# A four-layer decoder trunk on one core: the compressed branch of sparse attention in one 128x128 square under a rearranged plan, and differential attention pinned piece by piece

## The chip, the cores and the metric

The kernel runs on 1 core of one Trainium2 chip. The metric is device time in microseconds (us): the median of three runs of the kernel before is 2169.16 us (2161.97 to 2175.18). The engines of the core are TensorE (PE, matrix multiplications; PEld are its weight loads), VectorE (DVE), ScalarE (ACT), GpSimd (POOL) and SyncE (SP, which issues most DMAs). Each executes its own instructions in the order in which they were queued; they meet at semaphores.

## The reference

`x` is [1, 256, 1024], float32. Four layers, each `x + FFN_a/2`, `x + Mixer`, `x + FFN_b/2`, with norms and scales computed from a vector `c`. The mixers are NSA (layers 0 and 3), stick-breaking (layer 1) and differential attention (layer 2). Cut to the parts that the change touches:

```python
# NSA, compressed branch (15 blocks of 32 tokens; 16 heads in 4 groups)
s = einsum('bqgrd,bngd->bgrqn', q, k_cmp) * scale
s = where(dist >= 0, s - slopes * dist, NEG)             # dist = t - block end
p_cmp = softmax(s) * valid
o_cmp = einsum('bgrqn,bngd->bqgrd', p_cmp, v_cmp)
o = g[..., 0:1] * o_cmp + g[..., 1:2] * o_sel + g[..., 2:3] * o_win
return o @ w_out
# differential attention (8 heads, two maps each)
p = softmax(s - slopes * dist)
a = p[:, :, 0] - lam_full * p[:, :, 1]
o = rms_norm(einsum('bhqk,bkhe->bqhe', a, v), subln_g) * (1 - lam_init)
return o @ w_out
```

## The kernel before

Every weight matrix is streamed from memory in pieces and split into a high part (ScalarE, L135) and a low part (VectorE, L136); a product is three matmuls (high by high, low by high, high by low). One `lo_wo` or `lo_w` is such a VectorE subtraction of 128x1024. TensorE alternates between FFN stages and mixer stages. In the profiled execution NSA of layer 0 lies at 219 to 405 us of the span, NSA of layer 3 at 1803 to 1983, differential attention at 1291 to 1430.

A mixer is worked in four Attend pieces `a`, `b`, `c`, `d`: `a` and `b` hold the first eight heads for the first and the second 128 tokens, `c` and `d` the other eight (`HALVES`). In NSA each piece has the steps `S` (scores of two branches, L927; VectorE adds the distances and finds the row maximum with a fused custom instruction at L936; ScalarE takes the exponential; VectorE scales at L948), `T` (TensorE transposes the weights, ScalarE copies them as `pT`, L956 to L958), `P` (multiplied by the values, L909), `C` (compressed scores, L971, and their softmax on VectorE, L972 to L985), `D` (eight transposes of the compressed weights, 15 columns each, and two copies, L685 and L631), `E` (two matmuls with the compressed values `vc`) and `put` (output to `yh` and `yl`, L627 and L628). `q`, `kc`, `hid`, `cout`, `cout_T` make the projections and the compressed keys and values; `weight k` loads and splits a piece of the output weights, `o h k` multiplies by it.

The step strings in `plan` fix TensorE's order: `pin` (L304) makes each step's instructions come after the last matmul of the step before. The other engines' queues are laid by the scheduler from what TensorE's order and the data leave open. `bank` names three groups of PSUM banks: `acc` (4), `mm` (2; scores of `S` and `C`) and `tp` (2; transposes, and the projections in `cout_T`). A step that needs a bank waits until the last reader of that bank's previous content is done; so does one that needs an `s2` buffer (6, `NS2`).

Differential attention (`Diff`, a `Dense`) is not pinned: `plan` orders generator calls, and the scheduler mixes their instructions on TensorE: projections `proj`, `heads` (scores, L663, maximum L666), `second` (transposes L1145, values L1150), the normed output's transposes (`p_ot`, L1170) and `out_proj`.

Of the kernel before, what the change touches and what calls it, by code (L numbers as in the profile page):

```python
# [21 lines left out]
FT = mybir.dt.float32  # L22
FR = mybir.dt.float32r
BF = mybir.dt.bfloat16
AF = mybir.ActivationFunctionType
# [3 lines left out]
D = 1024  # L29
# [11 lines left out]
def trunk_kernel(ctx, tc, x, c, ada_w, ada_b, norm_g, ffn_w1, ffn_w2, nsa_w_in, nsa_cmp_pe, nsa_cmp_w1,  # L41
# [581 lines left out]

    def put_o(p, k0, h):

        tok = slice(h * 128, (h + 1) * 128)
        nc.scalar.copy(yh[:, k0:k0 + 4, tok], p)  # L627
        nc.vector.tensor_sub(yl[:, k0:k0 + 4, tok], p, yh[:, k0:k0 + 4, tok])  # L628
# [63 lines left out]
    class Nsa(Mixer):  # L692
        W = D + 6 * 256 + 48
        plan = """gate; q 0 0; gate_T; S a 0; q 0 2; S b 0 0; q 0 3; S b 0 1; kc 0 0; S a 1; T a 0 0; T a 0 1; kc 0 1;
                  P a 0 0; P a 0 1; kc 1 0; T b 0 0; T b 0 1; kc 1 1; P b 0 0; T b 0 2; q 1 4 0; P b 0 1; T b 0 3; q 1 4 1;
                  P b 0 2; P b 0 3; S b 1 0; q 1 5; S b 1 1; T a 1 0; T a 1 1; hid 0; P a 1 0; P a 1 1; S c 0; hid 1; weight 0;
                  hid 2; weight 1; hid 3; T b 1 0; T b 1 1; weight 2; q 1 2; P b 1 0; T b 1 2; weight 3; q 1 3 0; P b 1 1; T b 1 3; cout; q 1 3 1;
                  P b 1 2; P b 1 3; cout_T; S c 1; C a; T c 0 0; T c 0 1; C b; P c 0 0; P c 0 1; S d 0 0; D a; weight 4;
                  S d 0 1; E a; D b; weight 5; E b; o 0 0; C c; o 0 1; T c 1 0; T c 1 1; weight 6; o 0 2; P c 1 0; P c 1 1; S d 1 0;
                  o 0 3; D c; weight 7; C d; S d 1 1; E c; T d 0 0; T d 0 1; o 0 4; P d 0 0; T d 0 2; o 0 5; P d 0 1; T d 0 3;  # L700
                  o 0 6; P d 0 2; P d 0 3; o 0 7; D d; o 1 0 0; T d 1 0; E d; o 1 1 0; T d 1 1; P d 1 0; o 1 2 0; T d 1 2;
                  P d 1 1; o 1 3 0; T d 1 3; P d 1 2; P d 1 3; put d"""
        rest = """o 1 0 1; o 1 1 1; o 1 2 1; o 1 3 1; o 1 4 0; o 1 5 0; o 1 6 0; o 1 7 0; o 1 4 1; o 1 5 1; o 1 6 1; o 1 7 1"""

        def run(self, plan):


            for op in plan.replace("\n", " ").split(";"):
                op, *args = op.split()
                if args and args[0] in "abcd":  # L710
                    pin(getattr(self.at[args[0]], op), *map(int, args[1:]))
                else:
                    pin(getattr(self, op), *map(int, args))

        def body(self):
            pinned[:] = []
            self.at = {c: self.Attend(self, *half) for c, half in zip("abcd", HALVES)}
            self.run(self.plan)

        def tail(self):  # L720
            self.run(self.rest)
# [116 lines left out]
        def cout(self):  # L838
# [6 lines left out]
            self.hT = hT  # L845

        def cout_T(self):
# [9 lines left out]
            self.vc = work.tile([NCMP, 4, 64], FT, name="vc", tag="vc", bufs=1)  # L857
            p = bank("tp", [NCMP, 4, 64], "p_vc")
            for g in range(4):
                for cc in range(2):  # L860
                    nc.tensor.matmul(p[:, g, :], hT[:, cc, 64 + g * NCMP:64 + (g + 1) * NCMP], self.w2c[:, 1, cc, 0:64],
                                     start=cc == 0, stop=cc == 1)
            nc.scalar.copy(self.vc, p)
# [16 lines left out]
        def weight(self, k):  # L880
            gate_on[:] = self.copied
            self.wo[k] = self.out_weight(k)
            gate_on[:] = []

        def o(self, h, k, n=None):

            ns = (0, 1) if n is None else (n,)
            accs = self.accs.setdefault(h, [None, None])
            for m in ns:
                if accs[m] is None:  # L890
                    accs[m] = bank("acc", [128, 512], f"o{h}{m}")
# [397 lines left out]
```

## Time and profile before

| | us |
|---|---|
| median of three runs | 2169.16 |
| profiled execution | 2169.74 |
| its span | 2167.9 |
| PE busy in it | 2096.4 (97%) |
| DVE busy | 1622.9 (75%) |
| ACT busy | 1119.8 (52%) |
| NSA stage of layer 0, layer 3 | 185.7, 179.2 |
| differential attention | 139.4 |

The rows below come from four views: what TensorE waited for in a stretch, the busy time of the engines in stretches with the granted clock of TensorE (1.00 is 2.4 GHz, 0.50 would be 1.2 GHz throughout), groups of instructions by shape, and single instructions in order of time. In the rows `[1.53 <-DVE sm_m L936]` at the end of a row means that the engine had stood idle for 1.53 us and that the release came from VectorE's L936.

### The profile page before, as it was taken

The page shows a single profiled execution, that of the slowest core. Times are in us where ns is not written, and L with a number is a line of the kernel's source. Part 1 is how long each engine was busy: PE and PEld are TensorE (multiplying, and loading weights), DVE is VectorE, ACT ScalarE, POOL GpSimd, SP SyncE. Part 2 cuts the span into 40 slices and gives each one's busy share as a digit, 9 for nine tenths or more (in the row PEclk, how much of TensorE's full clock was granted, in tenths as well). Part 3 has the DMA queues.
Part 4 walks back from the last instruction along what each step waited for, and adds up shares of the span by engine and source line. Part 5 has one row for each costly group of instructions (what it writes and reads, how often), then busy time and mean ns, then how long its engine had stood idle before and what let it go on. Part 6 is the DMA issues. An engine that isn't in the chain of part 4 may idle for free.

```text
span 2167.9 us, 37376 instructions
## 1 busy us (share of the span) xinstructions
PE 2096.4 (97%) x14395; PEld 1856.1 (86%) x14395; DVE 1622.9 (75%) x2736; ACT 1119.8 (52%) x1989; POOL 67.3 (3%) x154
## 2 busy tenths in 40 slices
PE   5999999999999999999999999999999999999998
PEld 5999775899899979799989888789999997668998
DVE  7987866777798777677688858687779868767654
ACT  3444655644544456754464455664455445656443
POOL 1000000000000000100000000000000000000000
PEclk9999998999999999999999999999999999999999
DMA  9998752687699856388779958278869986545761
GB/s 316 335 348 287 252 137 78 215 287 262 199 330 312 282 186 222 122 278 277 256 235 330 313 170 297 78 240 274 275 203 330 308 276 194 163 118 172 241 200 59
DMA packets 338179, 512.55 MB, mean 236 GB/s; under 512 B 20832, under 2 KB 211256, under 8 KB 338000
## 3 DMA queue, kind: packets, MB, share of 16 engines
q1 hardware_dynamic: 329456, 501.15, 69.9%
q10 hardware_dynamic: 8544, 9.01, 1.4%
q8 instruction: 113, 1.85, 0.3%
q14 instruction: 66, 0.54, 0.1%
HBM read 507.91 MB, written 1.05 MB: 235 GB/s over the span
## 4 chain that ended last, share of the span: by engine, by line
PE 74%; DVE 11%; issue 5%; DMA 5%; ACT 4%; POOL 2%; ACTq 0%; SPq 0%; DVEq 0%; POOLq 0%
PE p_gu L386 12%; PE p_gu L388 12%; PE p_gu L387 12%; PE f L405 6%; PE f L406 6%; PE f L409 6%; DVE lo_w L136 3%; DMA raw_ada<-in_ada_w_dram 3%; PE p_o L909 1%; PE p_pr L386 1%; PE p_pr L387 1%; PE p_pr L388 1%; PE p_t L956 1%; POOL rx L325 1%; PE o L405 1%
## 5 line engine op out<-in xcount | busy, mean ns | idle before, releaser
L135 ACT CAST hi_w<-raw_w 128x1024 fp32r<-128x1024 f32 x528 | 551.5, 1055 | 325.6 <-PE f L409 113.4
L136 DVE TENSOR_TENSOR lo_w<-raw_w,hi_w 128x1024 fp32r<-128x1024 f32 x528 | 633.1, 1221 | 103.6 <-ACT hi_w L135 97.2
L386 PE MATMUL p_gu<-yh,hi_w 128*128 128x256 f32 x2368 | 665.6, 281 | 4.0 <-DVE yh L351 4.0
L387 PE MATMUL p_gu<-yl,hi_w 128*128 128x256 f32 x2368 | 660.9, 279 | 0.3 <-DVE yl L352 0.3
L388 PE MATMUL p_gu<-yh,lo_w 128*128 128x256 f32 x2368 | 661.0, 279 | 0.0
L386 PEld LDWEIGHTS p_gu<-yh,hi_w 128*128 128x128 f32 x2368 | 445.7, 188 | 17.3 <-DVE lo_w L136 6.2
L192 DVE SCALAR_TENSOR_TENSOR ada_acc<-raw_ada,cT,ada_acc 128x512 f32<-128x512 f32 x500 | 374.0, 749 | 103.3 <-DMA raw_ada<-in_ada_w_dram 95.3
L387 PEld LDWEIGHTS p_gu<-yl,hi_w 128*128 128x128 f32 x2368 | 446.0, 188 | 5.4 <-issue 1.7
L388 PEld LDWEIGHTS p_gu<-yh,lo_w 128*128 128x128 f32 x2368 | 445.8, 188 | 0.2
L405 PE MATMUL f<-hi_w,hb 128*128 128x512 f32 x704 | 275.8, 393 | 1.9 <-ACT hb L550 1.8
L406 PE MATMUL f<-lo_w,hb 128*128 128x512 f32 x704 | 275.9, 392 | 0.0
L409 PE MATMUL f<-hi_w,hb 128*128 128x512 f32 x704 | 228.3, 391 | 0.0
L550 ACT CAST hb<-sg 128x256 fp32r<-128x256 f32 x148 | 60.2, 407 | 199.6 <-DVE sg L549 198.1
L548 ACT ACTIVATE sg<-p_gu 128x256 f32<-128x256 f32 x148 | 56.3, 380 | 204.1 <-PE p_gu L388 183.8
L405 PEld LDWEIGHTS f<-hi_w,hb 128*128 128x128 f32 x704 | 132.3, 188 | 29.2 <-ACT hb L550 4.7
L409 PEld LDWEIGHTS f<-hi_w,hb 128*128 128x128 f32 x704 | 131.6, 188 | 29.3 <-DVE hb L551 1.9
L406 PEld LDWEIGHTS f<-lo_w,hb 128*128 128x128 f32 x704 | 132.2, 188 | 24.5 <-DVE lo_w L136 0.3
L549 DVE TENSOR_TENSOR sg<-sg,p_gu 128x256 f32<-128x256 f32 x148 | 61.5, 416 | 79.0 <-ACT sg L548 78.8
L551 DVE TENSOR_TENSOR hb<-sg,hb 128x256 fp32r<-128x256 f32 x148 | 62.4, 422 | 35.2 <-ACT hb L550 35.2
L350 ACT ACTIVATE y<-p_y,ab 128x128 f32<-128x128 f32 x184 | 67.2, 465 | 29.7 <-PE p_y L339 24.2
L387 PE MATMUL p_pr<-yl,hi_qk 128*128 128x256 f32 x256 | 71.8, 281 | 0.0
L386 PE MATMUL p_pr<-yh,hi_qk 128*128 128x256 f32 x256 | 71.5, 281 | 0.0
(273 smaller groups left out, 3191.6 us busy)
## 6 DMA issues: line engine op xcount, KB each, us to landing
raw_w<-in_ffn_w_dram SPq DMA_DIRECT2D x528, 512.0 KB
raw_ada<-in_ada_w_dram SPq DMA_DIRECT2D x288, 512.0 KB
raw_kv<-in_nsa_w_in_dram SPq DMA_DIRECT2D x16, 512.0 KB
raw_q<-in_nsa_w_in_dram SPq DMA_DIRECT2D x16, 512.0 KB
raw_cw<-in_nsa_cmp_w_dram SPq DMA_DIRECT2D x16, 512.0 KB
raw_wo<-in_nsa_w_out_dram SPq DMA_DIRECT2D x32, 256.0 KB
raw_qk<-in_sb_w_in_dram SPq DMA_DIRECT2D x16, 512.0 KB
raw_qk<-in_diff_w_in_dram SPq DMA_DIRECT2D x16, 512.0 KB
```

What stands on the lines that cost most here:

```text
L135: nc.scalar.copy(hi, src)
L136: nc.vector.tensor_sub(lo, src, hi)
L192: nc.vector.scalar_tensor_tensor(a, r[:, j], cT[:, k:k + 1], a, op0=OP.mult, op1=OP.add)
L350: nc.scalar.activation(y[:, j, :], p[:, j, :], AF.Identity, scale=ab[:, k:k + 1], bias=ab[:, 8 + k:9 + k])
L386: nc.tensor.matmul(o, cols(wh), yh[:, k, :], start=first and k == 0, stop=False)
L387: nc.tensor.matmul(o, cols(wh), yl[:, k, :], start=False, stop=False)
L388: nc.tensor.matmul(o, cols(wl), yh[:, k, :], start=False, stop=last and k == KC - 1)
L405: nc.tensor.matmul(acc[n], lh, wh[:, sl], start=first, stop=False)
L406: nc.tensor.matmul(acc[n], lh, wl[:, sl], start=False, stop=False)
L409: nc.tensor.matmul(acc[n], ll, wh[:, sl], start=False, stop=last)
L549: nc.vector.tensor_mul(sg, sg, p[:, 1, :])
L551: nc.vector.tensor_sub(hl[:, cc, :], sg, hh[:, cc, :])
```

## The change

It has three parts. (1) The compressed branch works on 16 columns for each of 8 heads, 128 in all, so that `D` is one 128x128 transpose and one copy; `E` becomes eight matmuls against `vz`, which holds the compressed values of a head's group in the rows of that head and zeros elsewhere (built in `cout_T` with the mask `own`). (2) The step string of NSA is rearranged. (3) `Diff` gets such a string, pinned step by step, in place of the generators. Line numbers of the kernel after are higher by 11 to 14 from L909 on.

```diff
 # NSA: cout, cout_T
+            hx = self.hx = s2([128, 2, 4, 4, 16], "hx")
+            nc.gpsimd.memset(hx, 0.0)
+            for cc in range(2):
+                nc.vector.tensor_copy(hx[:, cc, :, :, 0:NCMP], p[:, cc, 64:64 + 4 * NCMP].rearrange(
...
-                    nc.tensor.matmul(p[:, g, :], hT[:, cc, 64 + g * NCMP:64 + (g + 1) * NCMP], self.w2c[:, 1, cc, 0:64],
-            nc.scalar.copy(self.vc, p)
+                    nc.tensor.matmul(p[:, gp, :], self.hx[:, cc, 2 * gp:2 * gp + 2].rearrange("p e r n -> p (e r n)"),
+            for gp in range(2):
+                vz = self.X[0].rearrange("p m e -> p (m e)")[:, gp * 512:(gp + 1) * 512].rearrange("p (a d) -> p a d", a=8)
+                nc.vector.tensor_mul(vz, p[:, gp, None, :].to_broadcast([128, 8, 64]), own[:, :, None].to_broadcast([128, 8, 64]))
 # NSA: C, D, E
-                nc.vector.tensor_mul(m, m, self.nsa.gates[:, h, 8 * gp:8 * gp + 8, 0])
-                if not h:
-                    nc.vector.tensor_mul(pc, pc, cvalid[h][:, None, :].to_broadcast([128, 8, NCMP]))
+                nc.vector.scalar_tensor_tensor(m, m, cvalid[h][:, 0:1], self.nsa.gates[:, h, 8 * gp:8 * gp + 8, 0],
...
-                for e in range(2):
-                    self.ct[e] = transpose4(lambda rr: self.pc[:, 4 * e + rr, :], e)
+                p = bank("tp", [128, 128], "p_ct")
+                nc.tensor.transpose(p, self.pc.rearrange("p a n -> p (a n)"), ident)
+                self.ct = s2([128, 128], "cT")
+                evac(self.h, self.ct, p)
...
-                    self.add(e, slice(0, 4), self.nsa.vc[:, 2 * self.gp + e, :], self.ct[e][:NCMP])
+                for rr in range(4):
+                    for e in range(2):
+                        self.add(e, rr, self.nsa.vz[self.gp][:, 4 * e + rr, :], self.ct)
 # NSA: plan
-        plan = """gate; q 0 0; gate_T; S a 0; q 0 2; S b 0 0; ...
+        plan = """gate; q 0 0; gate_T; q 0 2; S a 0; q 0 3; S b 0 0; ...
 # Diff
-    class Diff(Dense):
+    class Diff(Pinned, Dense):
-        plan = [("proj", 1, 0,), ("proj", 0, 0,), 'a', ("proj", 1, 1,), 'b', 'a', ...
+        plan = """pj 1 0 0; pj 0 0 0; S a 0; pj 1 0 1 0; S b 0; pj 1 0 1 1; ...
...
+                  T c 0; pj 0 1 1 0; P c 0; weight 0; pj 0 1 1 1; N a; S c 1; T d 0; weight 1; N b; S d 1; P d 0; weight 2; o 0 0;
+                  weight 3; T c 1; o 0 1; weight 4; P c 1; T d 1; weight 5; o 0 2; weight 6; P d 1; o 0 3; weight 7; N c;
```

Three places in the instruction order. First TensorE in NSA, from the projections of `cout_T` (`p_kcT`, `p_vc`) to the first output product (`o_...`); `p_s` are the steps `S`, `p_sc` `C`, `p_t` from `sc` `T`, `p_t` from `pc` (after: `p_ct`) `D`, `p_o` from `pT` `P` and, from `vc` or `cT`, `E`. Before:

```order
L853 MATMUL p_kcT<-hT,self.w2c 128x60 x2
L861 MATMUL p_vc<-self.w2c,hT 15x64 x8
L927 MATMUL p_s<-qkv 128x256 x4
L971 MATMUL p_sc<-kc,qkv 128x32 x4
L956 MATMUL p_t<-ident,sc 128x128 x8
L971 MATMUL p_sc<-kc,qkv 128x32 x4
L909 MATMUL p_o<-pT,qkv 64x256 x4
L927 MATMUL p_s<-qkv 128x512 x2
L685 MATMUL p_t<-ident,pc 15x128 x8
L927 MATMUL p_s<-qkv 128x512 x2
L909 MATMUL p_o<-pT,vc 64x512 x2
```

The same stretch after, from the last `P` ahead of the scores of `d`:

```order
L920 MATMUL p_o<-pT,qkv 64x256 x4
L938 MATMUL p_s<-qkv 128x512 x2
L999 MATMUL p_ct<-ident,pc 128x128
L938 MATMUL p_s<-qkv 128x512 x2
L999 MATMUL p_ct<-ident,pc 128x128
L920 MATMUL p_o<-cT,qkv 64x128 x8
L938 MATMUL p_s<-qkv 128x256 x4
L920 MATMUL p_o<-cT,qkv 64x128 x8
L982 MATMUL p_sc<-kc,qkv 128x32 x4
L405 MATMUL o_3839<-hi_wo,yh 128x512
```

The scores `S c 1` (128x256 x4) moved from ahead of the first `C` to between `E a` and `E b`; `T c 0` now comes right behind `cout_T`, `C a` and `C b` stand together, and `C c` comes ahead of the first output product.

Second, VectorE's queue at the same place after: `L947 ISA` is the fused scores instruction (before L936), `L959` the scaling (before L948), `cT` the copy of `D a`, `yl` the output of a piece.

```order
L667 COPY cT<-p_ct 128x128
L136 TENSOR_TENSOR lo_wo<-raw_wo,hi_wo 128x1024
L954 RECIPROCAL sm_r<-sm_l 128x4
L947 ISA sc,sm_m<-p_s,dist 128x256
L947 ISA sm_m 128x1
L955 TENSOR_TENSOR sm_r<-sm_r,gates 128x4
L947 ISA sc,sm_m<-p_s,dist 128x256
L947 ISA sm_m 128x1
L959 TENSOR_SCALAR sc<-sc,sm_r 128x256 x4
L947 ISA sc,sm_m<-p_s,dist 128x256
L947 ISA sm_m 128x1
```

A weight split and four scalings stand between the fused instructions that read the scores of `d`, and the eight 128x128 ones of `S c 1` come behind all of these.

Third, TensorE in differential attention, where the projections are done and the output products begin: `p_ot` transposes a finished piece (step `N`), `p_t` the weights (`T`), `p_o` is the product with the values (`P`). Before:

```order
L1170 MATMUL p_ot<-ident,o_n 128x128 x2
L663 MATMUL p_s<-qkv 128x256 x7
L1170 MATMUL p_ot<-ident,o_n 128x128
L1145 MATMUL p_t<-ident,sc 128x128
L1170 MATMUL p_ot<-ident,o_n 128x128
L1145 MATMUL p_t<-ident,sc 128x128
L663 MATMUL p_s<-qkv 128x256
L1170 MATMUL p_ot<-ident,o_n 128x128 x2
L1150 MATMUL p_o<-qkv,aT 128x128 x2
```

After:

```order
L1220 MATMUL p_ot<-ident,o_n 128x128 x4
L699 MATMUL p_s<-qkv 128x128 x4
L1192 MATMUL p_t<-ident,sc 128x128 x4
L1220 MATMUL p_ot<-ident,o_n 128x128 x4
L699 MATMUL p_s<-qkv 128x256 x4
L1203 MATMUL p_o<-qkv,aT 128x128 x4
L405 MATMUL o_14988<-hi_wo,yh 128x512
```

The two last sets of scores of piece `d`, which stood together (x7 and x1 of 128x256), are apart: four of them here, the other four were moved up between the projections. The output products begin one `N` and one `P` after the last scores.

## Rows read from the trace of the kernel before

**Rows 1.** What TensorE waited for, NSA of layer 0 (219 to 405 us): total, times, longest.
```profile
PE p_o L909 <- DVE pT L631: 2.5, 1, 2.5
PE p_s L927 <- ACT qkv L775: 1.7, 1, 1.7
PE p_sc L971 <- DVE sm_m L936: 1.5, 1, 1.5
PE p_hid L824 <- DMA raw_cw<-in_nsa_cmp_w_dram: 1.0, 1, 1.0
PE p_o L909 <- ACT pT L958: 0.6, 1, 0.6
```

**Rows 2.** The same view, NSA of layer 3 (1803.5 to 1983 us).
```profile
PE p_hid L824 <- DMA raw_cw<-in_nsa_cmp_w_dram: 1.3, 1, 1.3
PE p_s L927 <- ACT qkv L775: 0.7, 1, 0.7
```

**Rows 3.** The same view, differential attention (1290.6 to 1430 us).
```profile
PE p_s L663 <- DVE sm_m L666: 4.3, 3, 2.4
PE o L405 <- ACT yh L627: 0.8, 1, 0.8
```

**Rows 4.** Stretches: length, busy PE, PEld, DVE, ACT, POOL, granted clock, DMA share, GB/s.
```profile
260.00:270.00 10.00, 9.16 (x56) 7.59 (x57) 8.02 (x39) 7.09 (x25) 0.00 (x0) 0.83 0.95 309
328.00:340.00 12.00, 11.35 (x51) 6.80 (x52) 8.94 (x50) 8.64 (x29) 0.00 (x0) 0.72 0.19 60
340.00:356.00 16.00, 13.48 (x51) 9.17 (x49) 9.26 (x33) 5.80 (x15) 0.00 (x0) 0.68 0.22 67
356.00:370.00 14.00, 14.00 (x68) 8.82 (x68) 11.77 (x42) 8.96 (x25) 0.00 (x0) 0.88 0.37 112
1380.00:1392.00 12.00, 9.63 (x41) 6.63 (x40) 9.07 (x36) 6.45 (x29) 1.01 (x1) 0.72 0.32 98
1920.00:1936.00 16.00, 13.48 (x52) 9.95 (x51) 9.00 (x30) 6.63 (x16) 0.00 (x0) 0.68 0.21 67
```

**Rows 5.** TensorE in order of time: `p_ht` and `S d 1 1`, layers 0 and 3.
```profile
321.67 0.38 PE L842 MATMUL p_ht<-ident,th 128*128 128x128 f32 x2
361.29 2.01 PE L927 MATMUL p_s<-qkv 64*128 64x512 f32 x4
...
1903.46 0.38 PE L842 MATMUL p_ht<-ident,th 128*128 128x128 f32 x2
1940.73 1.67 PE L927 MATMUL p_s<-qkv 64*128 64x512 f32 x4
```

**Rows 6.** VectorE by shape, NSA of layer 3: count, busy, mean ns, idle before.
```profile
L936 DVE CUSTOM_DVE_ANT_0 sc<-p_s,dist 128x256 f32<-128x256 f32 x32 | 12.2, 415 | 0.2 <-PE p_s L927 0.2
L136 DVE TENSOR_TENSOR lo_wo<-raw_wo,hi_wo 128x1024 fp32r<-128x1024 f32 x8 | 9.6, 1216 | 6.3 <-ACT hi_wo L135 6.3
L948 DVE TENSOR_SCALAR sc<-sc,sm_r 128x256 f32<-128x256 f32 x32 | 9.1, 347 | 0.2
L936 DVE CUSTOM_DVE_ANT_0 sc<-p_s,dist 128x128 f32<-128x128 f32 x32 | 7.1, 286 | 2.7 <-PE p_s L927 2.7
L628 DVE TENSOR_TENSOR yl<-p_o,yh 128x512 fp32r<-128x512 f32 x4 | 2.7, 684 | 3.7 <-ACT yh L627 3.7
```

**Rows 7.** VectorE in order of time, layer 3: first and last of the nine of `C c`.
```profile
1929.32 0.28 DVE L972 TENSOR_TENSOR pc<-p_sc,cdist 128x120 f32<-128x120 f32 x1 [3.04 <-PE p_sc L971]
...
1931.70 0.28 DVE L985 TENSOR_TENSOR pc<-pc,c_m 128x120 f32<-128x120 f32 x1
```

**Rows 8.** TensorE by shape, NSA of layer 3: `E` and `D` of four pieces.
```profile
L909 PE MATMUL p_o<-pT,vc 15*64 15x512 f32 x16 | 5.0, 640 | 2.5 <-DVE pT L631 2.5
L685 PE MATMUL p_t<-ident,pc 128*15 128x128 f32 x32 | 4.2, 273 | 0.3 <-DVE pc L985 0.3
```

**Rows 9.** TensorE by shape, the whole span: value products of layers 1 and 2.
```profile
L1090 PE MATMUL p_o<-sb_a,qkv 128*64 128x128 f32 x96 | 8.5, 281 | 1.4 <-POOL sb_a L1085 1.3
L1150 PE MATMUL p_o<-qkv,aT 128*128 128x128 f32 x48 | 6.9, 289 | 0.0
```

## What the change will do: the prediction

> **What bounds the kernel now.** I read four views, in this order. First, what TensorE waits for, stage by stage, because it is busy 97% of the span and only its gaps and its clock can be won. In the three stages touched it waits little: in NSA of layer 0 for the copies of the compressed weights (2.5), the first projected queries (1.7), the row maxima of scores (1.5), a weight load (1.0) and a copy of `pT` (0.6) [rows 1]; in layer 3 the 2.5, the 1.5 and the 0.6 are there again, the load takes 1.3 and the queries 0.7 [rows 2]; in differential attention it waits 4.3 for maxima and 0.8 for `yh` [rows 3]. Second, the granted clock: right after these waits it is below 1.00 [rows 4]. A stretch of length L at clock g was at the half level for 2(1-g)L: 3.4, 6.7, 10.2 and 3.4 us in layer 0, 10.2 in layer 3, 6.7 in differential attention. Half-level time costs at most half of itself. Third, VectorE's durations [rows 6, 7], since it is the engine waited for most. Fourth, single matmuls by shape, for what the square adds and removes [rows 8, 9].
>
> **The change part by part.** All is counted in the profiled execution (2169.7; 1.8 of it outside the span, untouched; 0.6 above the median).
>
> *A, the start of NSA.* `q 0 2` now stands between the first projection and `S a 0`. Its weights are those of `q 0 0`, already split, so it starts at once, and its 24 matmuls are longer than the wait for the queries. Layer 0 gains 1.7 [rows 1] and half of the 3.4 us at the half level that followed [rows 4]: 3.4. Layer 3, whose clock stayed up, gains 0.7 [rows 2].
>
> *B, the middle.* `S b 1 1` moved behind `T a 1`, so `pT` no longer stands behind its exponentials on ScalarE, and the four matmuls (about 1.1) cover the copy: 0.6 goes. The same matmuls stand ahead of `hid 0`, whose end frees the buffers of the load that `hid 3` waits for; the load starts later too, so of 1.0 and 1.3 I count 0.5 and 0.8. Gains 1.1 and 1.4; bounds 0 (the wait only moves) and 1.6 and 1.9.
>
> *C, from `p_ht` to `S d 1 1`*, where the square and the new order meet. Before, this took 361.3 - 321.7 = 39.6 us in layer 0 and 1940.7 - 1903.5 = 37.3 in layer 3 [rows 5]; `E c` stood behind it and now stands ahead, so I add its 5.0/16 x 4 = 1.25 [rows 8] to both: 40.9 and 38.5.
> TensorE's work: 37.3 less the waits 2.5, 1.5 and 0.3 and half of 10.2 at the half level [rows 1, 4, 8] is 27.9. Each `D` falls from 8 transposes to one: 4.2/32 x 8 = 1.05 [rows 8] becomes 0.13, for three pieces -2.8. Each `E` goes from two matmuls over 512 columns (1.25) to eight over 128 with 64 output rows; the nearest row, the same shape in layer 1, has 8.5/96 x 16 rows = 1.4 [rows 9]; the bounds are 1.1 (the old columns without half level) and 6.9/48 x 16 = 2.3, the shape of layer 2 with 128 output rows. I take 1.4, as its shape is the same: +0.2 for two pieces, +1.4 for `E c`. The projection of `vc` halves, -0.5. Sum 26.2, of which `D c` to `o 0 3` and `C d` are 8.2.
> VectorE's queue: where `D` was 1.05 us of cover, it is now 0.13, and `S d 0 1`, `S c 1`, `C c` and `D c` follow each other at distances shorter than VectorE needs. From the first subtraction of `C a` to the end of the softmax of `C c` it has: the softmaxes of `C a` and `C b`, 2.8; three weight splits, 3 x 1.2 = 3.6; a query scaling, 0.5; eight fused instructions on 256 columns, 8 x 0.38 = 3.0; eight scalings, 8 x 0.28 = 2.3; eight fused on 128, 8 x 0.22 = 1.8; eight scalings on 128 of the same length, 1.8; two `yl`, 1.3; copy and small ones, 0.8; and `C c` itself, 2.7 from 1929.32 to 1931.98 [rows 6, 7]. That is 20.6, against 18.0 of TensorE's work up to `D c`. The first subtraction comes 5.9 after `p_ht` (half a `q`, `P`s, the projections, `T c 0`, `C a`, and a wait of 0.9 at `T c 0 1` for the bank that the two `vz` products read); with overlaps of half a microsecond `D c` is at 26. TensorE then idles 7 to 8 us in several pieces, more than the 4.3 before, and `S d 1 1` comes at 26 + 8.2 = 34.2: 4.3 and 6.7 earlier. The half level after waits is hidden ahead of `D c`, where VectorE sets the pace, and costs after it; I count 2 us. Gains 4.7 in layer 0, 2.3 in layer 3. Bounds: if VectorE never held TensorE and the clock stayed up, 26.2 would stand, and the gains were 14.7 and 12.3; if all 8.2 after `D c` ran at the half level, 6.2 less each, a loss in layer 3.
>
> One rule of the Trainium skill speaks against this part: "TensorE: Matmul & The Clock Gate", section "A second HAM failure mode: psum-queue depth-cycling", says that a TensorE that idles briefly between groups while it cycles through PSUM banks makes its clock swing and loses throughput though single matmuls look fast. The trace agrees as far as the clocks of 0.72 and 0.68 behind such waits go [rows 4]. By the rule the pieces of idle time that I count would hold the clock down for longer than 2 us; what that would make is the third rival.
>
> *D, to the end of NSA.* `D d` -0.9, `E d` +0.2; layer 0 also had 3.4 us at the half level behind `S d 1 1` [rows 4], half of it 1.7. Gains 2.4 and 0.7. With `E` at its upper bound both `E c` and its sisters cost 0.9 more: 7 us over eight pieces.
> The same page, "Step-by-step: what each phase is for", says that the time of a matmul follows the columns streamed alone. By it `E`, 1024 columns before and after, would cost what it did, and the sum would be 1.2 us lower; the rows differ because narrow matmuls took longer per column here [rows 8, 9].
>
> *Differential attention.* Before: 4.3 + 0.8 idle and half of 6.7 at the half level, 8.5. After, `S d 0` and `S c 1` are spread, but from `N a` to `T d 1` VectorE has two `yl` (1.4), twelve fused score instructions (4 x 0.22 + 4 x 0.38 = 2.4 counting the eight that come here), the row sums and combinations of two score sets (about 2.5) and four weight splits (4.9), 11.2 in all, against 6.6 of TensorE. The shortfall of 4.6 appears ahead of `T c 1` and `T d 1`, with 0.6 behind `S d 1`: 5.2, and 1.5 for the clock. Gain 8.5 - 6.7 = 1.8; bounds 8.5 (all waits gone) and -3 (the clock low for twice as long).
>
> Sum: layer 0 3.4 + 1.1 + 4.7 + 2.4 = 11.6; layer 3 0.7 + 1.4 + 2.3 + 0.7 = 5.1; differential attention 1.8. Together 18.5: 2151.2, by the rounding of the half-level terms 2152.
>
> **Rivals.** *First, VectorE doesn't bind as I laid it* (same side). Its queue is ordered by what is ready, so a weight split may slip behind scores, and TensorE is then delayed by half as much. Then C gains 6.7 and 4.3 without the 2 us of clock, and differential attention 5.5: 3.4 + 0.7 + 2.5 + 11.0 + 3.1 + 5.5 = 26.2, 2143.5. For it: VectorE idles 3.04 us right after its dense stretch [rows 7], so it has room. Against it: two splits stand ahead of scores in the order after.
> *Second, the waits only move.* The clock falls in new places as often as in old ones and the load is as late as before; then B, C, D beyond -0.7 and differential attention give nothing but the shorter `D`, which VectorE's pace takes back, and A gives its waits alone, 1.7 + 0.7: 2167. For it: NSA of layer 3 did the same work with the same waits, but lost less clock [rows 4, 5], so what a wait costs is not fixed.
> *Third, slower: the half level through C.* One wait at `T c 0 1` or `S c 1` brings the clock down, and the short idle pieces that follow keep it there to `S d 1 1`. TensorE's 26.2 us then take 52.4, longer than VectorE's queue, instead of 34.2; 18.2 later in each layer, less the 2 counted: 2151.2 + 32.4 = 2184. It decides once 17 us of TensorE's work in each layer run at the half level; there the gain of 18 is used up. For it: 16.9 us of 328 to 356 were at the half level already, with less idle time [rows 4]. Against it: in layer 3 only 10.2 were.
>
> **How the numbers follow.** A measurement of this kernel tells about 0.5% (10.8 us) from no change: faster is under 2158.3, slower over 2180. My forecast has 0.49 with a range of its own from 2146 to 2158 (C and differential attention within 6 us together); the first rival 0.18; the second 0.25, counted as no change; the third 0.08. Faster 0.67, same 0.25, slower 0.08. The range reaches down past the first rival to 2140, and up to the second, 2168; outside lie the third and the ends of the two on either side, some 0.2.
>
> **What would show it.** A: no wait of the first scores for the queries, and a clock of 1.00 from 260 to 270. B: `P a 1 0` without wait, the wait of `hid 3` about 0.5. C: waits of `T c 0 1`, `S d 0 1`, `S c 1`, `C c` and `D c` on VectorE, 7 to 8 us in all, `S d 1 1` some 34 us after `p_ht` plus the clock's 2; `E` at 1.4 and `D` at 0.13. Differential attention: waits ahead of `T c 1` and `T d 1` of some 4.6 together, and none of 2.4 at scores. I am wrong in the size if VectorE's dense stretch is much under 20 us; in the kind if the granted clock from `S c 1` to `C d` is near 0.5, or if the pinned differential attention waits for its weights between projections, where nothing in the trace before shows a wait.

## The result: slower, by 0.58%

The changed kernel takes 2184.56 us in the median of 20 runs (2178.24 to 2190.01), the kernel before 2172.75 in as many; the ratio is 1.0058, 95% interval 1.0047 to 1.0068. The profiled execution has a span of 2182.8 us, 14.9 more than the one before. By stages (from the first `p_y` of a mixer's input to the `p_y` of the second 128 tokens of the next input): NSA of layer 0 fell from 185.7 to 180.0, NSA of layer 3 rose from 179.2 to 183.0, differential attention rose from 139.4 to 150.5, and all that the change does not touch, the FFN stages above all, rose by 5.7. TensorE was busy for 2093.0 us after and 2096.4 before, at a mean granted clock of 0.992 and 0.990: on balance, what was added is idle time.

A stage also varies from one execution to the next. The unchanged NSA stages of four kernels below (`e2_diff`, `e5_diff_nopin_pre`, `e6_diff_cover`, `e13_before_shift`) took 181.5 to 187.1 us in layer 0 and 180.4 to 184.9 in layer 3. So the 179.2 before is a short one, and a difference of 3 us in one stage of one profile shows little by itself.

What TensorE waited for after, NSA of layer 0 (total, times, longest), which answers to [rows 1]:

```profile
PE p_o L920 <- ACT pT L969: 3.7, 2, 2.5
PE p_hid L842 <- DMA raw_cw<-in_nsa_cmp_w_dram: 1.8, 2, 1.1
PE p_sc L982 <- DVE sm_m L947: 1.4, 1, 1.4
PE p_ct L999 <- DVE pc L995: 1.3, 2, 1.1
PE p_s L938 <- DVE sm_m L947: 1.0, 1, 1.0
...
PE p_t L967 <- ACT pT L969: 0.7, 1, 0.7
```

The waits for the queries (1.7) and for the 15-column copies (2.5) are gone. New is the first line: values `P` that wait for `pT`, and the load of `hid 3` is waited for longer than before. NSA of layer 3, which answers to [rows 2], has the same, larger:

```profile
PE p_o L920 <- ACT pT L969: 4.3, 2, 3.0
PE p_hid L842 <- DMA raw_cw<-in_nsa_cmp_w_dram: 3.6, 2, 2.4
PE p_ct L999 <- DVE pc L995: 2.9, 2, 2.7
PE p_s L938 <- DVE sm_m L947: 1.5, 2, 1.0
```

Differential attention, which answers to [rows 3]: the waits for maxima gave way to many others. (In this mixer the lines moved further than 11 to 14: scores from L663 to L699, transposes from L1145 to L1192, values from L1150 to L1203.)

```profile
PE p_y L339 <- DVE xn L355: 5.7, 2, 4.8
PE p_t L1192 <- DVE sc L1184: 3.1, 2, 2.0
PE p_o L1203 <- ACT aT L1194: 2.7, 2, 1.6
PE p_s L699 <- ACT qkv L1162: 2.0, 3, 1.0
PE p_s L699 <- DVE qkv L1163: 1.7, 2, 1.0
...
PE p_pr L1156 <- DVE lo_qk L136: 1.3, 1, 1.3
```

The granted clock by stretches (columns as in [rows 4]): the first stretch, 0.83 before, is at 1.00. In layer 0 it stays there from 270 to 336 us, through the waits for `pT` and for the load; in layer 3 (the rows at 1878 and 1908) it falls behind both. 336 to 352 lies where the two stretches at 0.72 and 0.68 were before.

```profile
260.00:270.00 10.00, 10.00 (x74) 8.53 (x73) 9.08 (x39) 6.91 (x24) 0.00 (x0) 1.00 1.00 312
270.00:336.00 66.00, 58.85 (x427) 43.11 (x425) 44.35 (x167) 35.19 (x102) 0.52 (x1) 1.00 0.55 145
336.00:352.00 16.00, 13.79 (x65) 9.09 (x65) 13.53 (x65) 8.93 (x36) 0.00 (x0) 0.68 0.24 74
352.00:360.00 8.00, 7.33 (x52) 5.13 (x52) 3.92 (x14) 4.39 (x10) 0.00 (x0) 1.00 0.13 34
1396.00:1424.00 28.00, 21.95 (x90) 17.55 (x91) 17.20 (x32) 16.14 (x43) 3.13 (x4) 0.82 0.36 113
1878.00:1886.00 8.00, 6.39 (x41) 5.83 (x42) 4.07 (x13) 2.17 (x9) 0.00 (x0) 0.79 0.00 0
1908.00:1916.00 8.00, 5.58 (x31) 3.42 (x30) 3.17 (x9) 1.94 (x4) 0.00 (x0) 0.79 1.06 218
```

### The profile page after: what moved, and what is told of

It is laid out like the page before. It is cut to its first block, busy times and chain, and to the rows that moved or that the text cites. A ratio compares the mean times of both kernels' runs of the same rounds, so it can differ in the third digit from the quotient of the medians.

```text
span 2182.8 us, 37444 instructions
## 1 busy us (share of the span) xinstructions
PE 2093.0 (96%) x14419; PEld 1858.9 (85%) x14419; DVE 1622.3 (74%) x2732; ACT 1115.7 (51%) x1987; POOL 67.3 (3%) x158
## 3 DMA queue, kind: packets, MB, share of 16 engines
HBM read 507.91 MB, written 1.05 MB: 233 GB/s over the span
## 4 chain that ended last, share of the span: by engine, by line
PE 74%; DVE 11%; issue 5%; ACT 5%; DMA 4%; POOL 2%; ACTq 0%; SPq 0%; DVEq 0%; POOLq 0%
PE p_gu L386 13%; PE p_gu L388 12%; PE p_gu L387 12%; PE f L405 6%; PE f L406 6%; PE f L409 6%; DVE lo_w L136 2%; PE p_o L920 1%; DMA raw_ada<-in_ada_w_dram 1%; POOL rx L325 1%; PE p_s L938 1%; PE o L405 1%; DVE ada_acc L192 1%; PE p_t L967 1%; PE o L409 1%
## 5 line engine op out<-in xcount | busy, mean ns | idle before, releaser
L953 ACT ACTIVATE sc<-sc,sm_m 128x256 f32<-128x256 f32 (+1 forms) x128 | 56.7, 445 | 25.1 <-DVE sm_m L947 24.2
L446 PE MATMUL p_gx<-hi_w,yh 128*128 128x256 f32 x224 | 63.3, 283 | 0.0
```

The costliest lines, as they stand in the source:

```text
L446: nc.tensor.matmul(p[:, 0], yh[:, k, tok], wg[k][0], start=st, stop=False)
```

## The experiments

All were timed against the kernel before on the same chip; ratios are to it. The groups below ran on different chips, so kernels of two groups are compared by their ratios. "NSA version" means differential attention as before.

**The parts alone.** `e1_nsa`: `class Diff` and its loop as before. `e2_diff`: the new `Diff` alone. `e3_square`: the NSA version with the old string. `e4_plan`: the new string with the old compressed branch.

```diff
-        plan = """gate; q 0 0; gate_T; q 0 2; S a 0; q 0 3; ...     # e3_square: old string
+        plan = """gate; q 0 0; gate_T; S a 0; q 0 2; S b 0 0; ...
```

> Both NSA parts of the change (square and rearranged plan), with differential attention as it was before. Theory 1 (the pinned differential attention is what made the kernel slower; NSA as a whole came out about even): in the two profiles the NSA stage of layer 0 fell from 185.7 to 180.0 us and that of layer 3 rose from 179.2 to 183.0, so this run is about 2 us faster than before, within 5 either way, and some 11 us faster than the full change; the differential stage is 139 to 140 us. Theory 2 (NSA carries the loss too, the differential stage in the profile after was an unlucky execution): 5 to 10 us slower than before.

> Differential attention pinned as in the change, NSA as before. Theory 1: the stage is 150 to 151 us long instead of 139.4, with the wait of p_y for xn of about 4.8 us at its end, and the kernel 11 us slower than before (ratio about 1.005). Theory 2: within 4 us of before.

> The 128-column square of the compressed branch under the old step string; differential attention as before. Theory 1 (the square is a gain, the new string is what loses in NSA): the wait for the copies of the compressed weights (2.5 us in each layer) is gone, each D is 0.9 us shorter, each E about 0.2 longer; 5 to 8 us less in each NSA stage, 10 to 15 faster than before. Rival (the square moves the wait to VectorE or costs in E as much as it saves in D): within 4 us of before.

> The rearranged step string with the old compressed branch (15-column copies, two wide matmuls in E); differential attention as before. Theory 1: the string alone loses: the copies pT of T a 0 stand behind the key shifts of kc 0 1 on ScalarE (waits of P of 3 to 4 us in each NSA stage) and the load for hid 3 is waited for 2 to 3.5; against it the first scores no longer wait; 4 to 10 us slower than before. Rival (the square carries the loss): 2 to 6 us faster than before, and no such waits.

Measured: `e1_nsa` 1.0029 (1.0010 to 1.0047), `e2_diff` 1.0040 (1.0025 to 1.0055), `e3_square` 1.0003 (0.9987 to 1.0020), `e4_plan` 1.0007 (0.9992 to 1.0022). Pinned differential attention costs 8.7 us, its stage is 150.4 long and ends with the 4.8 us wait, as theory 1 had it. The NSA version cost 6.3, the time that theory 2 gave. But in its profile the two NSA stages take 363.9 us together, against 364.9 before, as theory 1 had it, and 6.8 of the loss lie outside the three stages (1670.4 us there, 1663.6 before). Neither the square nor the string could be told from no change; the square's gain of 10 to 15 and the string's loss of 4 to 10 were both forecast wrong. The waits were as expected, though: 3.7 and 3.4 of `P` for `pT` in `e4_plan`, none above 0.5 in `e3_square`, where the 2.5 for the copies gave way to 1.4 and 1.6 for the new copy `cT`. Something cost the kernels with the square time that no wait shows.

**Differential attention.** `e5_diff_nopin_pre` and `e6_diff_cover` are `e2_diff` with one edit each:

```diff
-        (pin if isinstance(cur, (Pinned, Nsa)) else lambda f: f())(lambda: gate.extend(...    # e5
+        (pin if s == 1 and not i % 3 else lambda f: f())(lambda: gate.extend(...
...
-                  o 0 6; o 0 7; o 1 2 0; o 1 3 0"""                                           # e6; the eight leave `rest`
+                  o 0 6; o 0 7; o 1 2 0; o 1 3 0; o 1 0 1; o 1 1 1; o 1 2 1; o 1 3 1; o 1 4 0; o 1 5 0; o 1 6 0; o 1 7 0"""
```

> As the pinned differential attention alone (NSA as before), but the transposes of the next sub-layer's input (p_y) are no longer pinned ahead of the remaining output products. Theory (the pin is the largest piece of the loss): the wait of p_y for xn, 4.8 us with some 3 us of half level behind it, falls to under 0.5; the stage, 150.4 with the pin, is 143 to 145 long; 5 to 7 us faster than with the pin, 2 to 6 slower than before. Rival (TensorE has nothing left to do there, so the wait only moves to another instruction, or the loss is in the projections): stage 149 to 151.

> As the pinned differential attention alone, the pin kept, but eight half steps of the output product (o 1 0 1 to o 1 3 1 and o 1 4 0 to o 1 7 0) moved from behind p_y to ahead of it. Theory: eight times 0.7 = 5.6 us of cover hides the 4.8 us wait for xn; the stage is 143 to 145 long, as without the pin. Rival: as there, 149 to 151, or the later p_y holds up the next stage by as much (its first hidden products wait for y).

Measured: 1.0008 (0.9991 to 1.0024) and 1.0027 (1.0013 to 1.0041); the stages are 146.0 and 145.8 long. In the full change the transposes stood ahead of eight half steps that could have run:

```profile
1417.75 1.94 PE L339 MATMUL p_y<-ident,xn 128*128 128x128 f32 x8 [4.80 <-DVE xn L355]
```

The theory holds for the piece: 4.5 us of the stage's 11 are this wait, and eight half steps cover it. The stage stays 1 us longer than expected, since the other 6 remain. By the ratios `e5_diff_nopin_pre` gained 7.0 us on `e2_diff`; `e6_diff_cover` gained 2.8, which the intervals don't tell from nothing. The waits of `e5_diff_nopin_pre` name them:

```profile
PE p_t L1215 <- DVE sc L1207: 3.1, 2, 2.0
PE p_o L1226 <- ACT aT L1217: 2.6, 2, 1.5
PE p_s L663 <- ACT qkv L1185: 2.0, 3, 1.0
PE p_s L663 <- DVE qkv L1186: 1.7, 2, 1.0
```

**The string of NSA.** `e7_nsa_kc` is the NSA version with `kc` where it stood; `e8_nsa_kc_cw` also loads the first output weights later; `e9_splits_late` also moves three weight pieces.

```diff
-  q 0 3; S b 0 0; kc 0 0; S b 0 1; kc 0 1; S a 1; T a 0 0; T a 0 1; kc 1 0; P a 0 0; ...     # e7
+  q 0 3 0; S b 0 0; q 0 3 1; S b 0 1; kc 0 0; S a 1; T a 0 0; T a 0 1; kc 0 1; P a 0 0; ...
-  S c 0; hid 1; weight 0; hid 2; weight 1; hid 3; T b 1 0; T b 1 1; weight 2;                # e8
+  S c 0; hid 1; hid 2; hid 3; weight 0; T b 1 0; T b 1 1; weight 1; weight 2;
-  S d 0 0; weight 4; D a; ... E b; weight 5; C c; o 0 0; o 0 1; weight 6; D c; o 0 2; T c 1 0; T c 1 1; E c;   # e9
+  S d 0 0; D a; ... E b; C c; o 0 0; o 0 1; D c; o 0 2; T c 1 0; T c 1 1; weight 4; weight 5; weight 6; E c;
```

> Both NSA parts, differential attention as before, but the key projections kc stand where the old string had them: kc 0 1 behind T a 0 1, so that its copies and shift transfers on ScalarE come behind the copies pT and not ahead of them; the queries q 0 3 are cut into two halves to fill the place. Theory: the two waits of P for pT (3.6 and 3.4 us in the two NSA stages with the rearranged string) fall under 1; each NSA stage 3 to 4.5 us shorter than with the full string, 6 to 9 in all; 1 to 3 us faster than before. Rival (ScalarE's queue is late for its exponentials, whatever order kc has): waits of P stay above 2.5.

> As the run with kc moved back, and the output weight pieces 0 and 1 loaded behind hid 3 instead of between hid 1 and hid 3, so that the last two loads of the compression weights stand ahead of theirs in the queue of SyncE. Theory: the wait of hid 3 (2.0 and 4.2 us in the two stages) falls to about 1, 3 to 5 us less in all. Rival (the load is late because its buffers come free with the end of hid 0, not for the two transfers ahead of it): the wait falls by 1 at most; and the weight splits, later now, meet VectorE's dense stretch and lengthen the way from p_ht to S d 1 1 by 1 to 3 us.

> As the last NSA version (kc moved back, loads of hid 3 first; differential attention as before), but the output weight pieces 4 to 6 stand behind T c 1 1 in the string, so that two or three of their splits (1.2 us each) leave VectorE's dense stretch between C a and D c. Theory (VectorE's queue sets the time of D c): D c, 27.4 us after p_ht in that version, comes 1.2 to 2.4 earlier, the wait of p_ct (2.6 in layer 0, 1.1 in layer 3) falls to 0 to 1 and S d 1 1 (37.0 and 35.4 after p_ht) comes 1 to 2.4 earlier; 2 to 5 us less in all. Rival (the distance of dependent steps sets it, not the load of the queue): D c within 0.5 us of where it was, and the splits then stand in the way of D d and the last outputs.

Measured: 0.9985 (0.9972 to 0.9998), 0.9942 (0.9926 to 0.9958), 0.9951 (0.9933 to 0.9969). Against `e1_nsa` the first edit gained 4.4 thousandths (9.5 us), the second 4.3 more (9.3). In the profiles the two NSA stages fell together from 363.9 us to 356.2 (6 to 9 less were forecast) and then to 345.5: 10.7, where the theory had 3 to 5. ScalarE in the full change, layer 0, in order of time, shows what the first edit removed:

```profile
281.39 0.35 ACT L822 COPY ks<-p_kc 64x256 f32<-64x256 f32 x1
281.77 0.47 ACTq L825 DMA_DIRECT2D ks<-ks  x1
282.38 1.26 ACTq L826 DMA_DIRECT2D ks<-ks  x1
283.69 0.59 ACT L969 COPY pT<-p_t 128x512 f32<-128x512 f32 x1 [1.95 <-DVE sc L959]
...
286.87 0.57 ACT L969 COPY pT<-p_t 128x512 f32<-128x512 f32 x1
```

`kc 0 1` issues four shift transfers from ScalarE's own queue. In the new string it stands ahead of `T a 0`: ScalarE is idle for 1.95 us in front of the first `pT`, while its sequencer issues: the last issue took 1.26 and ended at 283.64, and the copy starts at 283.69. (The row names VectorE's scaling at L959 as what came last; the transposes that the copy reads were done by 281.6.) The second `pT` then comes behind seven exponentials. TensorE pays 2.48 for that:

```profile
287.49 0.65 PE L920 MATMUL p_o<-pT,qkv 128*64 128x256 f32 x4 [2.48 <-ACT pT L969]
```

In `e7_nsa_kc` the view of waits shows none of `P` for `pT`, in `e8_nsa_kc_cw` none for `raw_cw`: with the two output weight transfers out of its way the last load was issued 2.0 us after the start of `hid 0` in layer 3, not 3.9. In the full change the clock was down for 3.4 us behind both waits of layer 3 (the rows at 1878 and 1908).

Those two transfers stood ahead of the load in the kernel before too, and in both kernels they were issued 2.0 us after the start of `hid 0`. TensorE at `hid` in layer 3, before and after (`hid` was L824):

```profile
1883.92 1.95 PE L824 MATMUL p_hid<-raw_cw,qkv 128*64 128x256 f32 x16
1886.51 1.13 PE L909 MATMUL p_o<-pT,qkv 128*64 128x256 f32 x8 [0.63 <-ACT pT L958]
...
1894.09 1.94 PE L824 MATMUL p_hid<-raw_cw,qkv 128*64 128x256 f32 x14 [1.30 <-DMA raw_cw<-in_nsa_cmp_w_dram]
```

```profile
1899.12 1.95 PE L842 MATMUL p_hid<-raw_cw,qkv 128*64 128x256 f32 x16
1900.90 1.03 PE L920 MATMUL p_o<-pT,qkv 128*64 128x256 f32 x8
...
1907.75 0.65 PE L842 MATMUL p_hid<-raw_cw,qkv 128*64 128x256 f32 x2 [1.15 <-DMA raw_cw<-in_nsa_cmp_w_dram]
1910.81 0.69 PE L842 MATMUL p_hid<-raw_cw,qkv 128*64 128x256 f32 x2 [2.42 <-DMA raw_cw<-in_nsa_cmp_w_dram]
```

`P a 1 0` no longer waits 0.63 for `pT`, so TensorE comes to the load sooner; one wait became two. The place of the two transfers in the string did not change; what changed is how soon TensorE needs the load. The last load's wait ended 4.9 us after its issue before (issued at 1889.2) and 7.8 after (at 1903.0); why it took longer stays open. `e8_nsa_kc_cw` shows that the two transfers' place is enough to cure it.

`e9_splits_late` tests what holds `D c` in layer 3. First `e8_nsa_kc_cw`, then `e9_splits_late`, TensorE in order of time (`p_ht` at 1898.8 and 1898.4):

```profile
1926.22 0.33 PE L999 MATMUL p_ct<-ident,pc 128*128 128x128 f32 x1 [1.06 <-DVE pc L995]
...
1934.25 1.57 PE L938 MATMUL p_s<-qkv 64*128 64x512 f32 x4
```

```profile
1923.48 0.27 PE L999 MATMUL p_ct<-ident,pc 128*128 128x128 f32 x1
...
1932.00 1.05 PE L982 MATMUL p_sc<-kc,qkv 128*128 128x32 f32 x8 [1.29 <-DVE sm_m L947]
1932.98 1.12 PE L938 MATMUL p_s<-qkv 64*128 64x512 f32 x2
```

In layer 3 `D c` comes 2.3 us earlier without the splits, and without its wait: there VectorE's queue sets it. The splits then stand ahead of the maxima of `S d 1 0`, and `C d` gives back 1.3, the second half of `S d 1 1` another 0.5. In layer 0 the wait of `D c` (2.6) is gone too, but `D c` comes 0.4 us later, 27.8 after `p_ht`; the clock fell ahead of it there and not in `e8_nsa_kc_cw`. The time is the same; the 2 to 5 us of the theory did not come.

`e10_old_branch` has the string of `e8_nsa_kc_cw` and the old `C`, `D` and `E`.

> The same string as the version with kc moved back and the loads of hid 3 first, with the old compressed branch (transposes of 15 columns, copies of 15x512, two wide matmuls); differential attention as before. It tells what the square is worth by itself once the string doesn't stall. Theory: as the terms of D and E went, 3 us per layer of TensorE's work and VectorE's copies: this run is 4 to 8 us slower than the square under the same string. Rival (VectorE sets the pace there, and the square adds two broadcasts and two products to it): within 2 us.

Measured: 0.9915 (0.9898 to 0.9932), 2153.98 us: the square's kernel is not faster but 5.9 slower by the ratios. `S d 1 1` comes 36.7 after `p_ht` with the old branch, 37.0 and 35.4 with the square. The theory fell, and so did its rival's 2 us; between `p_ht` and `S d 1 1` the square neither gains nor costs.

`e11_diff2` puts a second pinned string for differential attention on `e8_nsa_kc_cw`. In it `N a` and `N b` write `yh` ahead of a projection that still reads it, so that part of the computation is changed.

> The NSA version with kc moved back and the loads of hid 3 first, and differential attention pinned by another string: both key halves before the queries, each S one projection half behind the copy of its operand, four output products between the last steps, eight half steps ahead of p_y. Theory (the loss of the pinned string is where scores stand right behind the projection that makes their operand, where values stand right behind the copy of the weights, and p_y): those waits (3.7, 2.6 and 4.8 us) go, the stage is 137 to 141 us, level with the unpinned one; the kernel within 4 us of the NSA version alone. Rival (a fixed order of TensorE can't do here what the scheduler's mixing does): stage 144 or longer, 5 to 8 us slower than the NSA version.

Measured: 0.9941 (0.9927 to 0.9955); the stage is 143.5 long, 3.6 of it waits of that projection for `yh` and `yl`.

**Where the buffers lie.** Outside the three changed stages the profiles of the kernels with the square take 1669.2 to 1672.3 us, those with the old branch 1663.0 to 1665.2. The average distance from one start of a `p_gu` matmul to the next (6996 distances of the trace under 600 ns) is 117.7 or 117.8 ns in every kernel with the old branch, 118.7 to 118.9 in every one with the square so far. The constants of the square are 32 bytes smaller, and all buffers allocated after them moved: in the built programs the first weight buffer starts at byte 48672 of a partition, before at 48704.

```diff
-        own = consts.tile([128, 8], FT, name="own")                       # e12, e14
+        own = consts.tile([128, 16], FT, name="own")[:, 0:8]
-        qscale = consts.tile([128, 8], FT, name="qscale")                 # e13, on the kernel before
+        qscale = consts.tile([128, 16], FT, name="qscale")[:, 0:8]
-        own = consts.tile([128, 8], FT, name="own")                       # e16: 32 columns, e17: 48
+        own = consts.tile([128, 32], FT, name="own")[:, 0:8]
```

> The full change with one unused block of 32 bytes behind the constant own, so that every later buffer lies 32 bytes higher, where it lay before the change; the order of all instructions is that of the full change. Theory (the smaller constants moved the weight buffers from a multiple of 64 bytes to 32 beyond one, and TensorE's matmuls follow each other about 1 ns later for it): start to start of the FFN's p_gu matmuls 117.7 ns instead of 118.7, the FFN stages together 5 to 6 us shorter, the kernel 4 to 7 us faster than the full change, at a ratio of about 1.003 to before. Rival (the FFN's longer stages come from the instructions around them, or by chance): 118.7 ns and a ratio of 1.005 to 1.006.

> The kernel before with the same block of 32 bytes behind its last constant, so that its weight buffers lie 32 bytes beyond a multiple of 64; nothing else. Theory: p_gu matmuls 118.7 ns apart instead of 117.7, p_gx about 114 instead of 117, the kernel 4 to 7 us slower than before (ratio about 1.0025). Rival: no difference (ratio within 0.0015 of 1, 117.7 ns).

> The NSA version with kc moved back and the loads of hid 3 first, square included, differential attention as before, with the 32 bytes. Theory: the square was not slower than the old branch under that string, its run only paid for the moved buffers; 4 to 7 us faster than without the bytes, 2152 to 2156, level with the old branch or up to 3 faster. Rival (the square itself costs): 2158 to 2161.

> The previous kernel with differential attention pinned by a mended string: both key halves before the queries, each S one projection half behind the copy of its operand, N a and N b behind the last projection (which reads the buffer that they write), output products between the last steps, eight half steps ahead of p_y. Theory: the stage is 138 to 141 us and the kernel within 3 us of the previous one. Rival: waits for VectorE at the end of the stage keep it at 143 or more, 3 us or more slower.

> As the NSA version with 32 bytes, but with 96 bytes: the weight buffers start at 48768 instead of 48704, again a multiple of 64, and now one of 128. Theory A (only the place within 64 bytes counts): p_gu matmuls 117 to 118 ns apart, the kernel at 2150 to 2154. Theory B (a longer pattern; four starts so far: 48672 gave 118.7, 48704 117.7, 48736 120.8): another spacing, 1 ns of it worth 7 us.

> The same with 160 bytes: the weight buffers start at 48832, 128 bytes above the version with 32 bytes. Theory A (place within 64 or within 128 bytes counts): the spacing and time of the version with 32 bytes, 117.7 ns and 2150 to 2154. Theory B (a longer pattern, or the distance to buffers that did not move): another spacing.

| first weight buffer | kernel | `p_gu` start to start | ratio |
|---|---|---|---|
| 48704 | `e12_after_pad`, the full change | 117.8 ns | 1.0047 (1.0030 to 1.0063) |
| 48736 | `e13_before_shift` | 120.8 | 1.0111 (1.0093 to 1.0130) |
| 48704 | `e14_nsa_pad`, 2151.36 us | 117.8 | 0.9920 (0.9904 to 0.9936) |
| 48704 | `e15_diff3`, 2152.47 us | 117.7 | 0.9926 (0.9910 to 0.9942) |
| 48768 | `e16_pad96` | 119.4 | 0.9962 (0.9950 to 0.9974) |
| 48832 | `e17_pad160` | 119.6 | 0.9973 (0.9962 to 0.9983) |

The clear case is `e13_before_shift`: 24 us slower than the kernel before beside it, with no instruction moved, where the theory had 4 to 7. With the 32 bytes the full change has the spacing of the kernel before again, and outside the three stages its profile takes 1664.2 us instead of 1669.2. Its time shows less: the ratio fell from 1.0058 to 1.0047, 2.4 us, which the intervals don't tell from nothing (`e14_nsa_pad` against `e8_nsa_kc_cw`: 4.8). Not every group moves alike: the median distance of the `p_gx` matmuls is 117 ns at 48704, but 114 at 48672 and 120 in `e13_before_shift`, where 114 was forecast. The page shows the effect in the matmuls, and in `e13_before_shift` in the weight load too (columns as in [rows 9]); first the kernel before, then the full change, then `e13_before_shift`:

```profile
L386 PE MATMUL p_gu<-yh,hi_w 128*128 128x256 f32 x2368 | 665.6, 281 | 4.0 <-DVE yh L351 4.0
L386 PEld LDWEIGHTS p_gu<-yh,hi_w 128*128 128x128 f32 x2368 | 445.7, 188 | 17.3 <-DVE lo_w L136 6.2
```

```profile
L386 PE MATMUL p_gu<-yh,hi_w 128*128 128x256 f32 x2368 | 668.9, 283 | 4.0 <-DVE yh L351 4.0
```

```profile
L386 PE MATMUL p_gu<-yh,hi_w 128*128 128x256 f32 x2368 | 674.6, 285 | 4.0 <-DVE yh L351 4.0
L386 PEld LDWEIGHTS p_gu<-yh,hi_w 128*128 128x128 f32 x2368 | 454.6, 192 | 17.3 <-issue 6.0
```

281 against 283 and 285 ns, and 188 against 192: over 7000 such matmuls the 3.1 ns of `e13_before_shift` are 21.7 us. Theory A of the last two runs fell: 128 bytes further on the spacing is another, 119.6, and the times are 2161.41 and 2163.93 us where 2150 to 2154 were forecast. Which placement is best, and why, stays open; every shift also changes the distance to `yh` and `yl`, which did not move.

`e14_nsa_pad` beats both kernels, the one before by 18 us: square, mended string, buffers where they lay. Its waits in NSA of layer 3 have no `pT` ahead of `P` and no load any more:

```profile
PE p_ct L999 <- DVE pc L995: 2.9, 2, 2.6
PE p_s L938 <- DVE sm_m L947: 1.5, 2, 1.0
...
PE p_sc L982 <- DVE sm_m L947: 1.1, 1, 1.1
```

It is level with the old branch under that string (0.9915): the 5.9 us of `e10_old_branch` were the bytes, as far as the intervals tell. It also means that the square by itself gains nothing that these runs can show. `e15_diff3`, with a pinned string that keeps scores and values away from the copies they need, has a stage of 141.9 us (138 to 141 were forecast) against 141.1 unpinned in `e14_nsa_pad`, and 139.3 to 143.6 in the profiles of all unpinned kernels; the times, 0.9926 and 0.9920, can't be told apart. So pinning as such was not what cost, the string was. Neither did it gain. Its remaining waits are at the end:

```profile
PE p_t L1193 <- DVE sc L1185: 2.6, 3, 1.5
PE p_ot L1221 <- DVE o_n L1216: 2.4, 1, 2.4
```

## Why the prediction was wrong, step by step

The forecast was 18 us faster; the kernel is 12 us slower. Three steps failed.

*Differential attention* (forecast a gain of 1.8): it costs 8.7, 11.1 in the profile. The shortfall that I did count, 4.6 at `T c 1` and `T d 1`, nearly came: 1.1 and 2.0 there, and 1.0 of `P c 1` between them, which waits for ScalarE's copy. What I left out is the pin on the next input's transposes, a line of the diff that I showed no cost for (4.5), and the waits where a step stands right behind the copy of its operand: scores behind projections (3.7) and `P c 0` behind `aT` (1.6). Before, the scheduler had put work there; a fixed order needs that work written into it. I also missed that all eight copies `aT` are on ScalarE after, where four were on VectorE; `e15_diff3` has them so too and doesn't pay, so that is not the cost by itself. My sign for being wrong in kind came as well: 1.3 us of waiting for a projection's low weights (`lo_qk`).

*B* (forecast gains of 1.1 and 1.4): I priced the steps that the string moves toward `hid`, and named no cost for `kc 0 1`, which it moves ahead of `T a 0`. Its four transfers go out through ScalarE's queue, past which I never followed `pT`. And for the load I counted what the matmuls moved ahead of `hid 0` would cover (0.5 and 0.8 gained), not that without the wait for `pT` TensorE comes to it sooner, with two output weight transfers still ahead of it: its wait rose from 1.0 and 1.3 us to 1.8 and 3.6. `P a 1 0` itself came without a wait, as forecast. Mending both took the ratio from 1.0029 to 0.9942, some 19 us. The waits that went are 13.2 of it (3.6 and 3.4 for `pT`, 2.0 and 4.2 for the load, in `e1_nsa`). The mean clock over the span rose from 0.992 to 0.994, which by these rounded means is some 9 us less at the half level and gives back up to 4.5; what is left lies within the intervals.

*Nothing outside the stages*: the sum had no term for the moved buffers. The 5.7 us there in the profile went back to 0.6 with the 32 bytes; in the times 2.4 of them show, within the intervals.

Right were: A, the wait for the queries gone and the clock at 1.00 from 260 to 270. C in the end nearly its size, and in part by luck: 0.7 waited at `T c 0 1` against 0.9 forecast (for ScalarE's copy `pT` by the row, not for the `vz` products), and waits at `D a`, `S d 0 1`, `C c` and `D c` on VectorE, 2.68 for the last in layer 3; `S d 1 1` 37.3 and 37.0 us after `p_ht`, against 34.2 and 2 for the clock. But the waits from `T c 0 1` to `D c` come to 4.5 and 5.7 us, not 7 to 8, and `D c` is at 29.3 and 28.9, not 26: the clock cost its time ahead of `D c`, where I had called that hidden, and nothing behind it, where I had put the 2. With `E c` counted on both sides, as there, the gains are 3.6 and 1.5, against 4.7 and 2.3. In these rows, which answer to [rows 5], 360.70 - 323.39 is that 37.3:

```profile
323.39 0.38 PE L860 MATMUL p_ht<-ident,th 128*128 128x128 f32 x2
...
360.70 1.15 PE L938 MATMUL p_s<-qkv 64*128 64x512 f32 x2
```

A smaller miss: at the full clock `E c` took 1.09 us after and 1.07 before, so `E` cost nothing, where I took 1.4 from layer 1's row. First after, then before:

```profile
1951.84 1.09 PE L920 MATMUL p_o<-cT,qkv 128*64 128x128 f32 x16
```

```profile
1942.33 1.07 PE L909 MATMUL p_o<-pT,vc 15*64 15x512 f32 x4
```

The Trainium skill ("TensorE: Matmul & The Clock Gate", "Step-by-step: what each phase is for") has a matmul's time follow the streamed columns alone, 1024 in both; these rows agree.

The third rival gave 2184, the measured time, and its mechanism is not what happened: in layer 0 the stretch from 336 to 352 was at 0.68, 10.2 us at the half level where 16.9 were before, and the way through C got shorter. The Trainium skill ("TensorE: Matmul & The Clock Gate", "A second HAM failure mode: psum-queue depth-cycling") has the clock swing under such short idle pieces, and the trace agrees: 0.68 from 336 to 352, and 1.00 again from 352 to 360 behind a wait of 1.05 at `D c`. The second rival's idea that waits move was nearest, but most moved to places that none of my rivals named, and the load it had as late as before, not later. That the string, mended in two places, and with the buffers back, gives the forecast's size (0.9920) shows that a gain of that size was to be had from the string, not that the forecast was sound: the old branch gives the same (0.9915), so the shorter `D`, the square's share of C, is not shown.

## What to carry to other kernels

When steps are written in a new order, follow each through every queue that it issues on, its transfers on a compute engine's queue above all, and ask of each step what stands between it and the copy of its operand. Where a scheduler's mixing is replaced by a fixed order, list the places where it had put filler, the hand-over to the next stage included. A change in the size of an early allocation, here of some constants, can change the time of matmuls that it has nothing to do with: compare the average start to start of an untouched group before explaining a difference by the edit.

## What was not expected of the hardware

32 bytes. Moving the weight buffers and all that is allocated behind them within a partition, with no instruction changed, moved the FFN's matmuls from 117.7 ns start to start to 118.7, 119.4, 119.6 or 120.8, and the kernel by up to 1.1% (`e13_before_shift`).
